# Feed-forward layers of a hybrid encoder block: where the row sums' pieces, the first down product and one weight part stand in the queues

## The chip, the cores and the metric

The kernel runs on one core of one Trainium2 chip. The metric is device time in microseconds (us) of one execution; the kernel before was run three times.

## The reference, cut to what matters

The whole block is a macaron: half a feed-forward layer, a mixer (convolution and gated linear attention), half a second feed-forward layer, and a gated per-layer input. The change touches the two feed-forward layers. In them, for 512 tokens, 1024 channels and an inner width of 2816:

```python
def _swiglu(x, w_in, w_out):
    gate, up = jnp.split(x @ w_in, 2, axis=-1)
    return (jax.nn.silu(gate) * up) @ w_out
h = h + 0.5 * _swiglu(_rmsnorm(h, ffn1_norm[i]), ffn1_w_in[i], ffn1_w_out[i])
...
h = h + 0.5 * _swiglu(_rmsnorm(h, ffn2_norm[i]), ffn2_w_in[i], ffn2_w_out[i])
```

## The kernel before, in words

Every float32 product is done as three matmuls of split operands: with a high part H and a low part L of each side, the kernel adds wH·xH, wH·xL and wL·xH. So every weight tile of 128x1024 values is fetched by SyncE (SP) into a raw tile `wr` (six buffers), cast by ScalarE (ACT) to `wh`, and its rest `wl` = `wr` − `wh` is made in one of two ways. `low` (line 193) makes it with one subtraction on VectorE (DVE). `added` (line 198) makes it without DVE: ACT writes −`wr`, rounded as `wh` is, into `wl` (a second ACT pass) and GpSimd (POOL) issues a DMA that adds `wr` to it in place.

The inner width is worked in pairs of 256 columns (11 pairs of 128-row blocks). Two kinds of pairs exist:

- A plain pair has eight units h0 to h7 on TensorE (PE), each of 12 matmuls of 512 columns. In the first layer pair 1 is plain. Its weight parts a11, a12 (gate) and a21, a22 (up) serve h0 to h3 and h4 to h7; h5 is the first user of a22.
- The others use a scheme with seven products instead of eight: units m1 (a11), m2 (a12), m6 (s2), m7 (s3), m5 (s1), m4 (a22), m3 (s4), each of 24 matmuls of 256 columns. s1 to s4 are sums of the weight parts (`sm` tiles, or written over `wr`), made by DVE. The other side needs sums over the tokens, too: t1 to t4.

Class `Right` (line 325 on) makes the token sums. `steps()` hands out five steps: pieces of `h` times a norm vector on ACT (`xg` tiles, four 128x256 activations a step) and differences of those on DVE. `split` turns the results into `t2H`, `t2L` and so on. Step 0 and 1 run ahead of the layer; steps 2 to 4 and the splits are hung on units as hooks, which run behind the unit's matmuls in program order.

`second(cut)` (line 749) makes the down products for a range of the inner width: four pieces, each of 2 x 12 matmuls of 512 columns with the activations `actH`, `actL` (made by `act_parts`, line 654, of `m`, the gated product of pair 0 and of pair 1) and a part of `w_out`.

The order on PE is the list `units`; `drive` (line 584) walks it. A unit's weight parts are fetched 7 to 9 units ahead and split 4 units ahead (`AHEAD`), or 6 units ahead where the unit stands in `adds`, which also sends its part through `added`. Each engine runs its instructions in the order in which the program issues them, so where a split stands in this walk is where it stands in the queue of ACT or DVE. Behind the plain pair the units before are: m1(2), m2(2), the first down piece, m1(3), m6(2), m7(2), m5(2), m2(3), m4(2), m3(2), the second down piece, m6(3) and so on; the number is that of the pair. All of these matmuls, splits and sums are recorded under line 46, that of a helper.

The second layer has no such list for its opening: lines 1436 to 1457 write it by hand. `plain_block` runs pair 0 as four blocks (g0, u0, g1_, u1_) between which the token sums and the first parts of pair 1 (`w1`) and pair 2 (`w2`) are made:

```python
    xb.split("t2", "t3")
    w1.part("s2")
    w1.add_part("a22")
    w2.add_part("a11")
    w1.s3_()
    u1_ = plain_block(w0, 1, 1)
```

Behind it come m1(1), m2(1), m1(2) and m6(1) on PE; m1(2) is the user of `w2`'s a11.

Of the kernel before, what the change touches and what calls it, by code (L numbers as in the profile page):

```python
# [62 lines left out]
def block_kernel(ctx: ExitStack, tc: tile.TileContext, a: dict, out: bass.AP):  # L63
# [195 lines left out]
    def spread(col, copy=True):  # L259

        ps = aux()
        for j in range(TB):
            pe.transpose(ps[:, j * P:(j + 1) * P], col[:, j:j + 1].to_broadcast([P, P]), ident)
        if not copy:
            return ps
        bc = tmp("bc", bufs=1)
        act.copy(bc, ps)
        return bc
# [245 lines left out]
    w1 = Left(ffn1_in, 2)  # L514
# [35 lines left out]
    xb = Right(hg, "ffn1_norm")  # L550
    steps = xb.steps()
# [4 lines left out]
    def constants():  # L556
        _, cwrow, gwurow = made
        gwu = cp.tile([P, 2 * P], F32, name="gwu")
        act.copy(gwu, gwurow)
        cw = cp.tile([P, 4 * WIDTH], F32, name="cw")  # L560
        ps = aux()
        for c in range(4):
            pe.transpose(ps[:, c * WIDTH:(c + 1) * WIDTH], cwrow[:, c * P:(c + 1) * P], ident[:WIDTH, :WIDTH])
        dve.tensor_copy(cw, ps[:, 0:4 * WIDTH])
        mean = cp.tile([P, P], F32, name="mean")
        pool.memset(mean, 1.0 / D_CONV)
        m1, m2 = (bt(s="m1")[:, 0:4 * CH].rearrange("p (c t) -> p c t", t=CH) for _ in range(2))
        mask = cp.tile([P, 4, CH], I32, name="mask")
        pool.memset(m1, 1.0)
        pool.memset(m2, 1.0)  # L570
        pool.affine_select(out=m1, in_=m1, compare_op=ALU.is_gt, fill=0.0, base=0,
                           pattern=[[0, 4], [-1, CH]], channel_multiplier=1)
        pool.affine_select(out=m2, in_=m2, compare_op=ALU.is_gt, fill=0.0, base=-CH,
                           pattern=[[0, 4], [-1, CH]], channel_multiplier=1)
        pool.tensor_copy(mask[0:CH], m1[0:CH])
        pool.tensor_copy(mask[CH:P], m2[CH:P])
        nbias = cp.tile([P, 2], F32, name="nbias")
        for j in range(2):
            dve.tensor_scalar(nbias[:, j:j + 1], vec("gate_b", j), -1.0, None, ALU.mult)
        made[:] = cw, gwu, mean, mask, nbias  # L580
# [23 lines left out]
    def ffn(w_in, w_out, x, gname, given, first, rsb, hooks, plain, adds=()):  # L604
# [6 lines left out]
        start = 1 + len(plain)  # L611
# [197 lines left out]
        units, had = [], set()  # L809

        def add(kind, i):
            if 0 <= i < npair and (kind, i) not in had:
                had.add((kind, i))
                units.append(unit(kind, i))

        cut_of = {f1 // 2 - 1: (f0, f1) for f0, f1 in CUTS}
        due = []
        for i in plain:
            for j in range(8):
                add(f"h{j}", i)  # L820
                if j in (2, 3, 5, 7):
                    units += due[:1]
                    due = due[1:]
# [1 line left out]
                due += second(cut_of[i])  # L825
        add("m1", start)
        add("m2", start)
        sooner, due = due[:1], due[1:]
        units += sooner
        add("m1", start + 1)  # L830
        for i in range(start, npair):
            add("m6", i)
            add("m7", i)
            add("m5", i)
            if i == end:
                half, rest = second(cut_of[i])
                units.append(half[0])
            else:
                add("m1", i + 1)
            add("m2", i + 1)  # L840
            if not (i == start and sooner):
                units += due[:1]
                due = due[1:]
            add("m4", i)
            add("m3", i)
            units += due[:1]
            due = due[1:]
            if i in cut_of and i < end:
                due += second(cut_of[i])
# [22 lines left out]
    def sums_hooks(x, names, at):  # L872

        h = {}
        for name, key in zip(names, at):
            h[key] = lambda *_, name=name: x.split(name)
        return h

    hooks = sums_hooks(xb, ("t2", "t3", "t1", "t4"), (("h4", 1), ("h5", 1), ("h6", 1), ("m1", 2)))
    hooks.update({("h%d" % (i + 1), 1): f for i, f in enumerate(steps[2:])})  # L880
    hooks.update({("m5", 3): lambda *_: made[0](), ("m5", 4): lambda *_: constants(),
                  ("m4", 10): lambda *_: w_ahead.append(ahead(w_in, D_CONV, 2 * P)),
                  ("last", 4): lambda *_: w_ahead.append(ahead(w_in, 0, 2 * P))})
    hg, norm = ffn(ffn1_in, a["ffn1_w_out"][0], xb, "mix_norm", {0: Left(ffn1_in, 0), 1: w1},
                   (ps0[:2], ps0[2:]), lambda: spread(mid[0]), hooks, (1,),
                   {("h4", 1), ("m1", 2), ("m4", 2)})
    pool.on = False
    cw, gwu, mean, mask, nbias = made

# [89 lines left out]
    for k0 in range(0, DC, 4):  # L979
        for i in range(2):  # L980
            for j in range(4):
                pe.matmul(ps[2 * RANK * j:2 * RANK * (j + 1)], gw[:, k0 + j, :], hg[k0 + j][i].bitcast(F32),
                          start=(k0 == i == 0), stop=(k0 + i == 5), skip_group_check=True)
# [339 lines left out]
    w0, w1 = wf[0], wf[1]  # L1323
# [100 lines left out]
    def plain_block(p, up, i, mid={}):  # L1424
        ps = bank()
        cs = slice(i * P, (i + 1) * P)
        for k in range(DC):
            if k in mid:
                mid[k]()
            wh, wl = p.part(f"a{1 + up}{1 + k // 4}")  # L1430
            mm3(ps, wh[:, k % 4, cs], wl[:, k % 4, cs], *hg[k], k == 0, k == DC - 1)
        return ps

    mid = []
    xb = Right(hg, "ffn2_norm")
    steps = xb.steps()
    steps[0]()
    w1.fetch("a21", "a22")
    w2 = wf[2]
# [8 lines left out]
    w1.s12()  # L1448
    g1_ = plain_block(w0, 0, 1, {1: lambda: mid.append(spread(mid[0]))})
    xb.split("t2", "t3")  # L1450
    w1.part("s2")
    w1.add_part("a22")
    w2.add_part("a11")
    w1.s3_()
    u1_ = plain_block(w0, 1, 1)
    xb.split("t1")
# [1 line left out]
    hooks = sums_hooks(xb, ("t4",), (("m2", 1),))  # L1458
# [3 lines left out]
    q11, q21, q12, q22, b11, b21, t2, wproj = ([] for _ in range(8))  # L1462
# [59 lines left out]
    def todo(*fs):  # L1522
# [6 lines left out]
                  ("rest", 4): todo((q_high, b21, q21, 1), (first_sum, 1), (third_sum, 1)),  # L1529
                  ("rest", 6): todo((final_in,), (row_sums, 0))})  # L1530
    hg, norm = ffn(ffn2_in, a["ffn2_w_out"][0], xb, "ple_norm", wf, ((g0, u0), (g1_, u1_)), mid[1], hooks, ())

    def of_rows(k, h):

        return [tuple(t[:, HS[h]] for t in hg[4 * k + c]) for c in range(4)]

    a11, a12, a21, a22 = of_rows(0, 0), of_rows(1, 0), of_rows(0, 1), of_rows(1, 1)
# [138 lines left out]
    def kept(ps, name, **kw):  # L1678
        o = tmp(name, **kw)
        act.copy(o, ps)  # L1680
        return o
# [20 lines left out]
    t1, t3 = q11, q12  # L1702
    n2_ = [x for jp in range(2) for x in split_rows(n2, jp)]
    project(0)
    m1 = [kept(p_, "sq", bufs=3) for p_ in x_]
# [98 lines left out]
```

## Time and profile before

| | us |
|---|---|
| median of 3 runs (lowest, highest) | 956.53 (956.1, 957.69) |
| the profiled execution's own time | 956.29 |
| its span in the profile | 954.6 |
| PE busy | 935.3 (98%) |
| DVE busy | 763.4 (80%) |
| ACT busy | 483.6 (51%) |

The span runs from the first to the last instruction; 1.69 us of the execution's own time lie around it. Starts are counted from the start of the span. A row of the timeline gives start, duration, engine, line, operation, tiles (numbers left out), shape, count, and in brackets how long the engine sat idle before it and what ended that. A matmul's duration overlaps the next one's, so the distance of starts is what it costs PE.

### The profile page before, as it was taken

To read this page: it belongs to the slowest core of one execution; us is meant where nothing else is said; L and a number is where in the kernel's file an instruction comes from. 1 tells how busy PE (TensorE), PEld (TensorE's weight loads), DVE (VectorE), ACT (ScalarE), POOL (GpSimd) and SP (SyncE) were. 2 spreads that over 40 slices of the span, in tenths; PEclk is the share of its full clock that TensorE was granted. 3 is DMA by queue.
4 is the path that set the end of the run, shared out by engine and by line. 5 is a ranking of instruction groups with operands and counts; after the bars stand their busy time and mean duration, and the time that the engine had idled before them with its cause. 6 is when DMAs were issued, how large, how long until landed. Compare 5 with 4: busy or idle time off the path is not lost.

```text
span 954.6 us, 14724 instructions
## 1 busy us (share of the span) xinstructions
PE 935.3 (98%) x5914; PEld 834.3 (87%) x5914; DVE 763.4 (80%) x1038; ACT 483.6 (51%) x728; POOL 56.9 (6%) x74
## 2 busy tenths in 40 slices
PE   9969999999999999999999999999999999999996
PEld 7859999999999988788877889999999999998885
DVE  6797778877878666999987689887888787865896
ACT  5863443344434473374564775444334443445882
POOL 0100010000000020101020010000000000000131
PEclk9989999999999999999999999999999999999998
DMA  7725232422243395338453554323243224347463
GB/s 227 207 61 154 74 101 92 133 89 90 89 133 94 108 245 131 89 67 200 99 121 112 135 114 128 111 91 104 94 133 102 77 89 133 95 139 225 94 111 110
DMA packets 108120, 114.48 MB, mean 120 GB/s; under 512 B 5187, under 2 KB 96501, under 8 KB 108052
## 3 DMA queue, kind: packets, MB, share of 16 engines
q1 hardware_dynamic: 101732, 94.67, 32.1%
q0 software_dynamic: 6304, 18.88, 11.0%
q8 instruction: 46, 0.75, 0.3%
q14 instruction: 22, 0.18, 0.1%
q10 hardware_dynamic: 16, 0.00, 0.0%
HBM read 93.61 MB, written 2.10 MB: 100 GB/s over the span
## 4 chain that ended last, share of the span: by engine, by line
PE 89%; DVE 4%; DMA 3%; ACT 2%; issue 2%; SPq 1%; POOL 0%; POOLq 0%; DVEq 0%; ACTq 0%
PE ps L46 88%; PE ax L46 1%; DMA wl<-wr 1%; DMA wr<-in_ffn_w_in 1%; DVE xg L46 1%; DVE wl L46 1%; DMA x<-in_x 1%; DVE sqacc L46 1%; ACT xg L46 1%; ACT wh L46 0%; DMA gwurow<-in_gate_w_up 0%; SPq L481 0%; ACT s L46 0%; DVE g L46 0%; SPq L446 0%
## 5 line engine op out<-in xcount | busy, mean ns | idle before, releaser
L46 PE MATMUL ps<-hgH,wl 128*128 128x256 f32 (+1 forms) x768 | 230.6, 305 | 1.4 <-DMA wl<-wr 1.4
L46 PE MATMUL ps<-hgH,wh 128*128 128x256 f32 (+1 forms) x768 | 231.5, 307 | 0.2 <-DVE wh L46 0.2
L46 PE MATMUL ps<-hgL,wh 128*128 128x256 f32 (+1 forms) x768 | 230.8, 306 | 0.0
L46 DVE TENSOR_TENSOR wl<-wr,wh 128x1024 fp32r<-128x1024 f32 (+2 forms) x161 | 188.6, 1182 | 46.6 <-ACT wh L46 46.5
L46 ACT CAST wh<-wr 128x1024 fp32r<-128x1024 f32 (+2 forms) x178 | 178.9, 1020 | 21.4 <-PE ps L46 6.9
L46 PEld LDWEIGHTS ps<-hgH,wh 128*128 128x128 f32 x768 | 146.5, 191 | 8.7 <-issue 1.1
L46 PEld LDWEIGHTS ps<-hgH,wl 128*128 128x128 f32 x768 | 146.7, 191 | 7.9 <-DMA wl<-wr 1.6
L46 PEld LDWEIGHTS ps<-hgL,wh 128*128 128x128 f32 x768 | 146.4, 191 | 6.9 <-issue 0.2
L46 PE MATMUL ps<-actL,wh 128*128 128x512 f32 x352 | 138.5, 394 | 6.5 <-DVE actL L46 6.5
L46 PE MATMUL ps<-actH,wh 128*128 128x512 f32 x352 | 138.6, 394 | 0.9 <-ACT actH L46 0.9
L46 PE MATMUL ps<-actH,wl 128*128 128x512 f32 x352 | 137.9, 392 | 0.0
L46 ACT ACTIVATE s<-g 128x512 f32<-128x512 f32 x48 | 30.4, 633 | 193.8 <-DVE g L46 193.8
L46 PEld LDWEIGHTS ps<-actL,wh 128*128 128x128 f32 x352 | 66.9, 190 | 19.4 <-DVE actL L46 6.8
L46 DVE SCALAR_TENSOR_TENSOR cv<-glu,cw,cv 128x502 f32<-128x502 f32 (+24 forms) x120 | 81.0, 731 | 0.6
L46 PEld LDWEIGHTS ps<-actH,wh 128*128 128x128 f32 x352 | 66.8, 190 | 14.3 <-ACT actH L46 1.3
L46 PEld LDWEIGHTS ps<-actH,wl 128*128 128x128 f32 x352 | 66.7, 190 | 14.1
L46 DVE SCALAR_TENSOR_TENSOR h<-ps,h 128x512 f32<-128x512 f32 x80 | 54.1, 686 | 20.2 <-PE ps L46 20.2
L46 ACT COPY sq<-ps 128x512 f32<-128x512 f32 x42 | 24.5, 586 | 79.6 <-PE ps L46 79.4
L46 DVE TENSOR_TENSOR wl<-sm,wh 128x1024 fp32r<-128x1024 f32 x42 | 51.0, 1220 | 1.8 <-ACT wh L46 1.6
L46 ACT CAST wh<-sm 128x1024 fp32r<-128x1024 f32 x42 | 43.7, 1043 | 5.6 <-DVE sm L46 3.4
L46 DVE TENSOR_TENSOR u<-ps,sq 128x512 f32<-128x512 f32 x19 | 13.1, 691 | 39.3 <-ACT sq L46 39.3
L46 ACT CAST actH<-m 128x512 fp32r<-128x512 f32 x44 | 25.3, 618 | 37.9 <-DVE m L46 37.7
(267 smaller groups left out, 1815.2 us busy)
## 6 DMA issues: line engine op xcount, KB each, us to landing
wr<-in_ffn_w_in SPq DMA_DIRECT2D x84, 512.0 KB
wr<-in_ffn_w_out SPq DMA_DIRECT2D x32, 512.0 KB
wr<-in_w_in SPq DMA_DIRECT2D x20, 512.0 KB
wl<-wr POOLq DMA_DIRECT2D x18, 512.0 KB, 5.6
wr<-in_ffn_w_out SPq DMA_DIRECT2D x16, 384.0 KB
wr<-in_w_out SPq DMA_DIRECT2D x8, 512.0 KB
wq<-in_ple_w_gate SPq DMA_DIRECT2D x8, 512.0 KB
wl<-wq POOLq DMA_DIRECT2D x8, 512.0 KB, 4.6
```

The lines of the kernel that those rows point to most:

```text
L46: inst = call(*args, **kwargs)
```

## The change

In the first layer the units lose the early place of the first down piece: it now stands behind m2(3), like those of later pairs. Steps 2 and 3 of the token sums move to the hook of h0 (they were on h1 and h2), step 4 to h1 (it was on h3), and the splits of t2, t3 and t1 to h2, h3 and h4 (they were on h4, h5, h6). The part a12 of pair 2 goes through `added`, 6 units ahead, as its a11 and a22 did already. In the second layer `w2`'s a11 and `w1`'s a22 are made ahead of s2 of `w1`, and a11 first.

```diff
         add("m1", start)
         add("m2", start)
-        sooner, due = due[:1], due[1:]
-        units += sooner
         add("m1", start + 1)
...
             add("m2", i + 1)
-            if not (i == start and sooner):
-                units += due[:1]
-                due = due[1:]
+            units += due[:1]
+            due = due[1:]
             add("m4", i)
...
-    hooks = sums_hooks(xb, ("t2", "t3", "t1", "t4"), (("h4", 1), ("h5", 1), ("h6", 1), ("m1", 2)))
-    hooks.update({("h%d" % (i + 1), 1): f for i, f in enumerate(steps[2:])})
+    hooks = sums_hooks(xb, ("t2", "t3", "t1", "t4"), (("h2", 1), ("h3", 1), ("h4", 1), ("m1", 2)))
+    hooks.update({("h0", 1): lambda *_: [f() for f in steps[2:4]], ("h1", 1): steps[4]})
...
-                   {("h4", 1), ("m1", 2), ("m4", 2)})
+                   {("h4", 1), ("m1", 2), ("m2", 2), ("m4", 2)})
...
+    w2.add_part("a11")
+    w1.add_part("a22")
     w1.part("s2")
-    w1.add_part("a22")
-    w2.add_part("a11")
     w1.s3_()
```

ACT in the first layer, behind the split of the first activations (`actH`), before. `wr_429` is a22 of pair 1 (for h5), `wr_479` a11 of pair 2:

```order
L46 CAST wh_481<-wr_429 128x1024
L46 ACTIVATE xg_497<-h_97,vcol_93 128x256
L46 ACTIVATE xg_497<-h_98,vcol_93 128x256
L46 ACTIVATE xg_500<-h_97,vcol_93 128x256
L46 ACTIVATE xg_500<-h_98,vcol_93 128x256
L46 CAST wh_508<-wr_479 128x1024
L46 ACTIVATE wl_509<-wr_479 128x1024
L46 ACTIVATE s_515<-g_113_513 128x512
L46 ACTIVATE xg_530<-h_101,vcol_93 128x256
```

The same place now; `wr_429` is still a22 of pair 1 and `wr_495` a11 of pair 2:

```order
L46 ACTIVATE xg_479<-h_97,vcol_93 128x256
L46 ACTIVATE xg_479<-h_98,vcol_93 128x256
L46 ACTIVATE xg_482<-h_97,vcol_93 128x256
L46 ACTIVATE xg_482<-h_98,vcol_93 128x256
L46 ACTIVATE xg_488<-h_101,vcol_93 128x256
L46 ACTIVATE xg_488<-h_102,vcol_93 128x256
L46 ACTIVATE xg_491<-h_101,vcol_93 128x256
L46 ACTIVATE xg_491<-h_102,vcol_93 128x256
L46 CAST wh_497<-wr_429 128x1024
L46 CAST wh_522<-wr_495 128x1024
L46 ACTIVATE wl_523<-wr_495 128x1024
```

All eight pieces now stand ahead of the cast that h5 needs; before, none did.

DVE in the first layer from the split of t2 on, before. `wl_586` is a12 of pair 2 (for m2), `wl_614` the part of `w_out`, `m_619` the product of pair 1:

```order
L46 TENSOR_TENSOR t2L_578<-xg_422,t2H_577 128x512
L46 TENSOR_TENSOR t2L_582<-xg_533,t2H_581 128x512
L46 TENSOR_TENSOR wl_586<-wr_506,wh_585 128x1024
L46 TENSOR_TENSOR t3L_602<-xg_416,t3H_601 128x512
L46 TENSOR_TENSOR t3L_606<-xg_500,t3H_605 128x512
L46 TENSOR_TENSOR sm_609<-wr_537,wr_539 128x1024
L46 TENSOR_TENSOR sm_610<-sm_609,wr_479 128x1024
L46 TENSOR_TENSOR wl_614<-wr_541,wh_613 128x1024
L46 TENSOR_TENSOR u_139_617<-ps_564,bc_454 128x512
L46 TENSOR_TENSOR m_619<-u_139_617,s_515 128x512
```

The same place now; `wl_622` is a11 of pair 3 (for m1(3)), `m_627` the product of pair 1:

```order
L46 TENSOR_TENSOR t3L_576<-xg_482,t3H_575 128x512
L46 TENSOR_TENSOR g_131_579<-ps_531,bc_454 128x512
L46 TENSOR_TENSOR t1L_597<-xg_413,t1H_596 128x512
L46 TENSOR_TENSOR t1L_601<-xg_479,t1H_600 128x512
L46 TENSOR_TENSOR sm_604<-wr_516,wr_518 128x1024
L46 TENSOR_TENSOR sm_605<-sm_604,wr_495 128x1024
L46 TENSOR_TENSOR wr_516<-wr_495,wr_516 128x1024
L46 TENSOR_TENSOR wl_622<-wr_552,wh_621 128x1024
L46 TENSOR_TENSOR u_142_625<-ps_583,bc_454 128x512
L46 TENSOR_TENSOR m_627<-u_142_625,s_529 128x512
```

The subtractions for a12 of pair 2 and for `w_out` have left this stretch of DVE; the token splits, all three weight sums and a11 of pair 3 now stand ahead of `m`.

ACT in the opening of the second layer, before. `wr_5370` is a22 of pair 1, `wr_5372` a11 of pair 2, `sm_5478` s2 of pair 1:

```order
L46 CAST t3H_5525<-xg_5411 128x512
L46 CAST wh_5529<-sm_5478 128x1024
L46 CAST wh_5533<-wr_5370 128x1024
L46 ACTIVATE wl_5534<-wr_5370 128x1024
L46 CAST wh_5538<-wr_5372 128x1024
L46 ACTIVATE wl_5539<-wr_5372 128x1024
L46 CAST t1H_5569<-xg_5362 128x512
```

The same place now; `wr_5373` is a11 of pair 2, `wr_5371` a22 of pair 1, `sm_5479` s2:

```order
L46 CAST t3H_5526<-xg_5412 128x512
L46 CAST wh_5530<-wr_5373 128x1024
L46 ACTIVATE wl_5531<-wr_5373 128x1024
L46 CAST wh_5535<-wr_5371 128x1024
L46 ACTIVATE wl_5536<-wr_5371 128x1024
L46 CAST wh_5540<-sm_5479 128x1024
L46 CAST t1H_5570<-xg_5363 128x512
```

a11 of pair 2 has moved from the last of three to the first, and POOL's two adding DMAs follow in the same new order.

## Prediction

> **What bounds the kernel now.** I read the page first: PE is busy for 98% of the span, so what can be won is PE's idle time and its time at a low clock. The list of waits of PE then says who caused it; two entries are of the stretches that the change touches.
>
> ```profile
> PE 935.3 (98%) x5914; PEld 834.3 (87%) x5914; DVE 763.4 (80%) x1038; ACT 483.6 (51%) x728; POOL 56.9 (6%) x74
> PE ps L46 <- DVE actL L46: 6.5, 1, 6.5
> PE ps L46 <- DMA wl<-wr: 1.4, 1, 1.4
> ```
>
> The timeline of PE shows the first place. The rows are: the third product of h5, two products of the plain pair 17 apart, the first and last product of m1(2) and m2(2), the down piece up to its two waits, and the first product back at full pace.
>
> ```profile
> 46.02 0.39 PE L46 MATMUL ps<-hgH,wl 128*128 128x512 f32 x1
> ...
> 49.65 0.39 PE L46 MATMUL ps<-hgH,wh 128*128 128x512 f32 x1
> ...
> 53.50 0.39 PE L46 MATMUL ps<-hgH,wl 128*128 128x512 f32 x1
> 53.73 0.28 PE L46 MATMUL ps<-hgH,wh 128*128 128x256 f32 x1
> ...
> 59.36 0.28 PE L46 MATMUL ps<-hgH,wl 128*128 128x256 f32 x1
> ...
> 60.64 0.39 PE L46 MATMUL ps<-actH,wl 128*128 128x512 f32 x1
> 61.91 0.50 PE L46 MATMUL ps<-actH,wh 128*128 128x512 f32 x1 [0.88 <-ACT actH L46]
> 68.88 0.80 PE L46 MATMUL ps<-actL,wh 128*128 128x512 f32 x1 [6.47 <-DVE actL L46]
> ...
> 74.45 0.40 PE L46 MATMUL ps<-actH,wl 128*128 128x512 f32 x1
> ```
>
> A product of 512 columns costs (53.50 − 49.65) / 17 = 0.227 us, one of 256 costs (59.36 − 53.73) / 47 = 0.12, so a unit of 24 costs 2.88. At that pace the product of 61.91 was due at 60.87 (1.04 late), the one of 68.88 at 62.14 (6.74 late), and the 13 steps from there to 74.45 took 5.57 instead of 2.95 (2.62 late). The first place costs **10.40**.
>
> The 2.62 are clock: the windows by stretch show it at 0.67 on average while PE waits. With full clock up to some moment and half clock behind it that moment is 64.0.
>
> ```profile
> 50.00:55.00 5.00, 5.00 (x29) 4.34 (x28) 3.55 (x6) 3.98 (x7) 0.00 (x0) 1.00 0.00 1
> 55.00:60.00 5.00, 5.00 (x42) 4.91 (x41) 4.97 (x6) 4.04 (x6) 0.00 (x0) 1.00 0.00 0
> 62.00:68.00 6.00, 0.41 (x1) 0.09 (x1) 5.97 (x10) 1.08 (x2) 0.00 (x0) 0.67 0.38 122
> 574.00:575.00 1.00, 0.06 (x1) 0.00 (x0) 0.76 (x2) 1.00 (x2) 0.00 (x0) 1.00 0.97 224
> ```
>
> Why the activations are late is in DVE's timeline: none of these rows has idle time before it, and `actL` of pair 1 stands behind splits and sums that only later units need.
>
> ```profile
> 58.41 1.22 DVE L46 TENSOR_TENSOR wl<-wr,wh 128x1024 fp32r<-128x1024 f32 x1
> 59.54 0.68 DVE L46 TENSOR_TENSOR u<-ps,bc 128x512 f32<-128x512 f32 x1
> 60.26 0.69 DVE L46 TENSOR_TENSOR m<-u,s 128x512 f32<-128x512 f32 x1
> 60.87 1.28 DVE L46 TENSOR_TENSOR t1L<-xg,t1H 128x512 fp32r<-128x512 f32 x2
> ...
> 63.21 1.22 DVE L46 TENSOR_TENSOR wl<-wr,wh 128x1024 fp32r<-128x1024 f32 x1
> 64.34 1.22 DVE L46 TENSOR_TENSOR wl<-sm,wh 128x1024 fp32r<-128x1024 f32 x1
> ...
> 66.19 0.69 DVE L46 TENSOR_TENSOR m<-u,s 128x512 f32<-128x512 f32 x1
> 66.80 1.42 DVE L46 TENSOR_TENSOR hgL<-xg,hgH 128x256 fp32r<-128x256 f32 x4
> 68.14 1.28 DVE L46 TENSOR_TENSOR actL<-m,actH 128x512 fp32r<-128x512 f32 x2
> ```
>
> By starts, a long DVE step costs 1.13, a short one 0.60, and 0.12 more where it needs the one before; they are readable 1.22 and 0.69 after their start.
>
> **First layer: what the change removes.** The down piece leaves this place, so both waits for `act` and the slow clock go: 10.40. Behind m2(3), 5 units of 2.88 later, its activations are due near 76 and, by the walk below, ready at 71. The question is what PE waits for instead.
>
> **First layer: the new queue.** ACT's prices are read from these rows, POOL's from the two below:
>
> ```profile
> 40.86 1.05 ACT L46 CAST wh<-wr 128x1024 fp32r<-128x1024 f32 x1
> 41.81 1.70 ACT L46 ACTIVATE xg<-h,vcol 128x256 f32<-128x256 f32 x4
> 43.42 1.04 ACT L46 CAST wh<-wr 128x1024 fp32r<-128x1024 f32 x1
> ...
> 51.02 0.63 ACT L46 ACTIVATE s<-g 128x512 f32<-128x512 f32 x1 [2.87 <-DVE g L46]
> 51.55 1.12 ACT L46 CAST t2H<-xg 128x512 fp32r<-128x512 f32 x2
> 52.58 1.05 ACT L46 CAST wh<-wr 128x1024 fp32r<-128x1024 f32 x1
> ...
> 45.73 0.86 POOL L46 DMA_DIRECT2D wl<-wr  x1 [9.19 <-ACT wl L46]
> DMA to landing us min/median/max: 5.0/5.0/5.0
> ```
>
> So 0.95 a long cast, 0.40 a piece, 0.53 a silu, 0.52 a short cast, and 5.0 from POOL's issue to landing; the pass before it ended at 43.42 + 0.95 + 1.05, so POOL issues 0.3 behind ACT. I walk the new order from 40.86, where before the cast for h5 began; nothing ahead of it has moved.
>
> 1. ACT runs eight pieces (8 x 0.40) to 44.1 and casts a22 until 45.15; DVE's subtraction ends at 46.4. h5's third product was at 46.02: it waits **0.5**. Bounds: none, if pieces run at 0.35, to 0.6.
> 2. ACT makes a11 of pair 2 until 47.0 (its DMA lands at about 52.3, needed at 54.4). DVE does three differences and the gate product (0.60, 0.72, 0.60) until 48.9; ACT follows with silu, t2 (2 x 0.52) and the two passes of a12, which end at 52.5. POOL issues 0.3 later, landing is at 57.8. m2(2)'s third product is due at 53.73 + 0.5 + 2.88 + 0.24 = 57.35: it waits **0.5**. Before, DVE had made this part in time; that is the price of the move to POOL. The other row for such a DMA is 7.85 (the chain, below), from a moment with fetches and another adding DMA in flight. I take 5.0, since both windows from 50 to 60 show the DMA idle, and the one fetch that moves ahead (a12 of pair 3, behind DVE's subtraction) starts at 46.4. With 7.85 the wait would be 3.4.
> 3. ACT: t3 until 53.6, silu at 55.0 behind DVE's gate product, t1 until 56.7, cast of a11 of pair 3 until 57.6. DVE: t1 at 56.2 and 56.8, the three sums at 57.4, 58.6, 59.8, then `wl` of a11 at 60.9, ready at 62.1. m1(3)'s third product is due at 57.9 + 2.64 + 0.24 = 60.8: it waits **1.4**. This and the wait before share their cover: a later landing lengthens one and shortens the other, to 3.4 together at the most and 1.9 at the least.
> 4. DVE goes on with u, m, and the splits of s2, s1, s3 at 63.35, 64.5, 65.6. m6(2) needs s2 at 65.1 and has it at 64.6: **0**, with 0.5 of cover; m7(2) and m5(2) have over 1 us. The second `m` ends at 68.2; ACT then casts `actH`, the two passes of a22 and a12 of pair 3 until 71.7, DVE has its rest at 72.9, needed at 73.7: **0**.
> 5. Two dependent gate steps on DVE end at 74.2, ACT's silu and copy at 75.3, the cast of the `w_out` part at 76.3, its rest at 77.6. The down piece's third product is due at 62.2 + 2.64 + 4 x 2.88 + 0.45 = 76.8: it waits **0.8** (none, if step 3 is 0.8 later).
>
> New waits: 0.5 + 0.5 + 1.4 + 0.8 = 3.2, between 2.4 and 4.3. Walked the same way, the old order gives 68.5 for the product of 68.88. From m4(2) on both orders are the same on PE, and no wait of that kind stands in PE's list between there and the second layer, so the time kept stays kept.
>
> **Second layer.** ACT's row of s2 and of the last pass, the chain's piece for the DMA, and PE:
>
> ```profile
> 562.40 1.05 ACT L46 CAST wh<-sm 128x1024 fp32r<-128x1024 f32 x1 [1.46 <-DVE sm L46]
> ...
> 566.20 1.06 ACT L46 ACTIVATE wl<-wr 128x1024 fp32r<-128x1024 f32 x1
> 567.56 7.85 DMA wl<-wr
> 573.78 0.28 PE L46 MATMUL ps<-hgL,wh 128*128 128x256 f32 x1
> 575.45 0.39 PE L46 MATMUL ps<-hgH,wl 128*128 128x256 f32 x1 [1.39 <-DMA wl<-wr]
> 575.67 0.28 PE L46 MATMUL ps<-hgH,wh 128*128 128x256 f32 x1
> ```
>
> m1(2) waits from 573.90 to 575.45, and the next step takes 0.22 instead of 0.12: 1.65. Now a11's two passes take the place in which ACT sat idle for 1.46 (from 560.9) and end at 562.9; POOL issues at about 563.4, and landing is at 568.4 to 571.3 by 5.0 and 7.85: the wait goes, with 2.6 us to spare. What is queued behind: s2's cast. It must wait for a `wh` buffer that u1_ reads until the middle of its 24 products, near 573.66 − 2 x 2.88 − 12 x 0.227 = 565.2, so DVE's subtraction for s2 is done at about 567.5; m6(1) needs it near 576.8, after 9 us of other products. The next sums slip by half a microsecond on DVE and are needed later still. Gain **1.65**, none of it at the least.
>
> **The sum.** Four restarts at 0.1, by the same two rows, add 0.4 to the new waits: 3.6. So 956.29 (the profiled execution's own time) − 10.40 + 3.6 − 1.65 = 947.84, say **947.8**. The median of the runs is 0.24 above that execution; the difference goes into the range. About 0.2% (1.9 us) is what a measurement of this kernel can tell from no change.
>
> **Rivals.**
>
> - *The clock falls again.* Before, it fell at 64.0, 1.6 us after the last product ended, with only one product in the 3 us before. A wait of 1.55 at 573.9 amid products left it at 1.00. If a new wait near 2 us or over drops it, 13 steps again cost 2.6: 950.4. It decides when the m2(2) and m1(3) waits fall together, by a landing past 7 us. [...] I give 0.12.
> - *DVE is the bound, and the wait only changes its name.* DVE is full for 9 us before `actL`, and the order of its work is all that changes; m6(2) has but 0.5 of cover. If DVE runs 3 us later than walked (a long step at the 1.25 of a dependent one, ACT answers late), s2 is late by 2.5: 950.3. Against it: two long steps (a12 of pair 2, the `w_out` part) have left the stretch. 0.09.
> - *The second layer gains nothing* because s2 or t1 becomes the late one: 947.8 + 1.65 = 949.5. 0.04.
> - *Slower than before.* a22 of pair 2 is added by POOL at 71.0, and only its landing frees the raw buffer into which a22 of pair 3 is fetched. The sum s1 of pair 3 waits for that on DVE, ahead of the split of s4 for m3(2). With a landing of 7 and a fetch of 4 (an estimate: it moves the bytes that take 5.0 there) s4 is ready near 85.6, and m3(2) needs it at 85.8: no cost. Each microsecond beyond is one of PE, and past some 3 the clock falls, too (2.6). It ends slower than before by over 1.9 us from 8 us longer than that on: with 8.4, 947.8 + 8.4 + 2.6 = 958.8. No row shows a landing over 7.85. 0.05.
>
> **How the numbers follow.** The forecast has 0.70, at 947.8, between 945.5 (waits of 2.4, restarts hidden, m1(3) helped by faster steps) and 949. The first four cases are faster, 0.95 together; 0.01 of them I leave for two of their losses at once, which ends within 0.2%. The last case is slower, but for 0.01 of its 0.05 in which its delay stays short of that: faster 0.94, within 0.02, slower 0.04. The range 945.3 to 950.8 holds the forecast, the clock case, the second-layer case and most of the DVE case.
>
> **What would show it.** Right: no idle for `actL` at the down piece, which stands near 76; PE rows with waits of half a microsecond at h5 (DVE `wl`) and m2(2) (DMA `wl`), over 1 us at m1(3) (DVE `wl`), under 1 us at the down piece; clock 1.00 from 50 on; no DMA wait in m1(2) of the second layer. Wrong: a clock row under 1.00 between 55 and 80, waits at m6(2) or m3(2), or PE's wait for the adding DMA of a12 over 2 us.

## The result: a little slower, and where the wait went

The changed kernel takes 958.37 us in the median (957.23 to 960.09, 13 runs) against 956.42 for the kernel before, run beside it; the ratio is 1.0023 [1.0014, 1.0031]. The prediction was 947.8, in a range of 945.3 to 950.8, with 0.94 for faster: wrong in size and sign.

TensorE (PE) of the changed kernel, from the page and from its list of waits (columns of the list: who waits, for whom, us in total, times, longest):

```profile
PE 936.5 (98%) x5914; PEld 835.7 (87%) x5914; DVE 762.8 (80%) x1037; ACT 484.9 (51%) x729; POOL 57.7 (6%) x75
PE ps L46 <- ACT u L46: 8.0, 2, 6.1
PE ps L46 <- DVE wl L46: 1.9, 2, 1.7
```

The entries for DVE `actL`, ACT `actH` and the DMA are gone, as forecast. In their place stands one that the kernel before has not at all: PE waits twice for ScalarE's (ACT's) `u`, 8.0 us together. The timeline of PE shows both, and the two waits for a weight's low part. The row of PEld, PE's weight load, is that of m2(2)'s third product:

```profile
46.55 0.39 PE L46 MATMUL ps<-hgL,wh 128*128 128x512 f32 x1
47.21 0.50 PE L46 MATMUL ps<-hgH,wl 128*128 128x512 f32 x1 [0.27 <-DVE wl L46]
...
58.35 0.19 PEld L46 LDWEIGHTS ps<-hgH,wl 128*128 128x128 f32 x1 [0.24 <-DMA wl<-wr]
...
61.22 0.28 PE L46 MATMUL ps<-hgL,wh 128*128 128x256 f32 x1
63.15 0.38 PE L46 MATMUL ps<-hgH,wl 128*128 128x256 f32 x1 [1.65 <-DVE wl L46]
...
71.52 0.28 PE L46 MATMUL ps<-t3H,wl 128*128 128x256 f32 x1
77.86 0.58 PE L46 MATMUL ps<-t1H,wh 128*128 128x256 f32 x1 [6.06 <-ACT u L46]
...
83.15 0.31 PE L46 MATMUL ps<-hgH,wh 128*128 128x256 f32 x1
...
583.93 0.28 PE L46 MATMUL ps<-t3H,wl 128*128 128x256 f32 x1
586.11 0.38 PE L46 MATMUL ps<-t1H,wh 128*128 128x256 f32 x1 [1.90 <-ACT u L46]
```

By starts, with 0.227 and 0.12 as a step at full pace: h5 loses 47.21 − 46.55 − 0.227 = 0.43, m1(3) 1.93 − 0.12 = 1.81, m5(2) 6.34 − 0.12 = 6.22. The 24 products of m5(2) take 83.15 − 77.86 = 5.29 instead of 2.88, another 2.41. The second layer's m5(1) loses 2.18 − 0.12 = 2.06. m2(2) loses 0.20 for the adding DMA of a12, too little for the list. The restarts at h5, m2(2), m1(3) and m5(1) add 0.1 each: the step behind the wait takes 0.33 instead of 0.227 at h5, and 0.22 or 0.23 instead of 0.12 at the others. Together 13.5 come; 10.40 and 1.65 went. That is 1.5 of the 2.2 us between the two spans. Another 0.8 was there before the first changed instruction (the last section), so the account closes to 0.1.

The products slowed at m5(2) are the clock again. Windows of the changed kernel by stretch; the number behind POOL's is the granted clock:

```profile
75.00:76.00 1.00, 0.00 (x0) 0.00 (x0) 1.00 (x2) 0.73 (x2) 0.00 (x0) 1.00 1.03 197
76.00:77.00 1.00, 0.00 (x0) 0.00 (x0) 0.38 (x1) 1.00 (x2) 0.00 (x0) 0.69 0.02 0
77.00:82.00 5.00, 4.14 (x19) 4.14 (x20) 2.94 (x3) 1.76 (x3) 0.00 (x0) 0.50 0.67 209
82.00:84.00 2.00, 2.00 (x14) 2.00 (x13) 1.87 (x2) 0.62 (x2) 0.00 (x0) 0.70 0.01 2
```

What `u` is, the code says. m6 and m5 work in the same PSUM bank `p.x`, and ACT must copy what stands there after m6 (`u2`) before m5 may add to it:

```python
        def m6(p):
            mul(p.x, p.part("s2"), x.op["t2"], False, False)
            p.u2 = snap(p.x, "u2", bufs=1)
        def m5(p):
            mul(p.x, p.part("s1"), x.op["t1"], False, False)
```

m6(2)'s last product started at 68.64; the copy ran at 77.22. ACT's timeline of the changed kernel shows what stood ahead of it in the queue:

```profile
65.47 0.62 ACT L46 CAST actH<-m 128x512 fp32r<-128x512 f32 x1
69.19 0.62 ACT L46 CAST actH<-m 128x512 fp32r<-128x512 f32 x1 [3.10 <-DVE m L46]
69.72 1.05 ACT L46 CAST wh<-wr 128x1024 fp32r<-128x1024 f32 x1
70.67 1.05 ACT L46 ACTIVATE wl<-wr 128x1024 fp32r<-128x1024 f32 x1
71.63 1.03 ACT L46 CAST wh<-wr 128x1024 fp32r<-128x1024 f32 x1
75.27 0.63 ACT L46 ACTIVATE s<-g 128x512 f32<-128x512 f32 x1 [2.62 <-DVE g L46]
75.81 0.57 ACT L46 COPY sq<-ps 128x512 f32<-128x512 f32 x1
76.28 1.05 ACT L46 CAST wh<-wr 128x1024 fp32r<-128x1024 f32 x1
77.22 0.59 ACT L46 COPY u<-ps 128x512 f32<-128x512 f32 x1
```

ACT isn't busy; it is held, for 3.10 us by VectorE's (DVE's) `m` and for 2.62 by its `g`, and the copy, which needs neither, stands behind both. The late `m` and `g` are the same DVE queue that delayed `actL` before. In the second layer it is the same picture: the copy is the second instruction behind a silu that waited 3.79 us for `g`.

```profile
584.47 0.63 ACT L46 ACTIVATE s<-g 128x512 f32<-128x512 f32 x1 [3.79 <-DVE g L46]
585.01 0.57 ACT L46 COPY sq<-ps 128x512 f32<-128x512 f32 x1
585.47 0.59 ACT L46 COPY u<-ps 128x512 f32<-128x512 f32 x1
```

The kernel before has the same two copies, and no wait for them. Its copies and first products of m5(2) and m5(1):

```profile
81.33 0.59 ACT L46 COPY u<-ps 128x512 f32<-128x512 f32 x1 [2.29 <-PE ps L46]
84.02 0.28 PE L46 MATMUL ps<-t1H,wh 128*128 128x256 f32 x1
...
583.19 0.59 ACT L46 COPY u<-ps 128x512 f32<-128x512 f32 x1
583.95 0.28 PE L46 MATMUL ps<-t1H,wh 128*128 128x256 f32 x1
```

There the copy ended 2.1 us ahead of m5(2), which came some 12 us later than in the new order, but only 0.17 us ahead of m5(1).

**The theory** to test: PE's wait wasn't removed but moved, from the activations at the down piece to the copy of `u2` at m5, because ACT works in order and something that waits for DVE stands ahead of the copy. **Rivals**: VectorE as a whole is the bound, so that the wait returns under any name; or one of the other parts (earlier pieces, one more adding DMA) is the cost.

### The profile page after: what moved, and what is told of

It is laid out like the page before. It is cut to its first block, busy times and chain, and to the rows that moved or that the text cites. A ratio compares the mean times of both kernels' runs of the same rounds, so it can differ in the third digit from the quotient of the medians.

```text
span 956.8 us, 14725 instructions
## 1 busy us (share of the span) xinstructions
PE 936.5 (98%) x5914; PEld 835.7 (87%) x5914; DVE 762.8 (80%) x1037; ACT 484.9 (51%) x729; POOL 57.7 (6%) x75
## 4 chain that ended last, share of the span: by engine, by line
PE 92%; DVE 4%; ACT 3%; issue 1%; POOLq 0%; POOL 0%; ACTq 0%; DVEq 0%
PE ps L46 90%; PE ax L46 1%; ACT wh L46 1%; DVE wl L46 1%; DVE g L46 1%; ACT xg L46 1%; ACT s L46 0%; ACT wl L46 0%; DVE m L46 0%; ACT sq L46 0%; DVE sm L46 0%; DVE xg L46 0%; DVE t1L L46 0%; DVE u L46 0%; DVE wr L46 0%
## 5 line engine op out<-in xcount | busy, mean ns | idle before, releaser
L46 PE MATMUL ps<-hgH,wl 128*128 128x256 f32 (+1 forms) x768 | 230.9, 306 | 2.0 <-DVE wl L46 1.9
L46 PE MATMUL ps<-hgH,wh 128*128 128x256 f32 (+1 forms) x768 | 232.5, 308 | 0.0
L46 PE MATMUL ps<-hgL,wh 128*128 128x256 f32 (+1 forms) x768 | 230.9, 306 | 0.0
L46 DVE TENSOR_TENSOR wl<-wr,wh 128x1024 fp32r<-128x1024 f32 (+2 forms) x160 | 187.5, 1182 | 47.5 <-ACT wh L46 47.4
L46 ACT CAST wh<-wr 128x1024 fp32r<-128x1024 f32 (+2 forms) x178 | 179.3, 1021 | 18.7 <-issue 6.7
L46 PEld LDWEIGHTS ps<-hgH,wl 128*128 128x128 f32 x768 | 146.8, 191 | 9.2 <-DVE wl L46 2.5
L46 PEld LDWEIGHTS ps<-hgH,wh 128*128 128x128 f32 x768 | 147.1, 192 | 8.6 <-issue 1.1
L46 PEld LDWEIGHTS ps<-hgL,wh 128*128 128x128 f32 x768 | 146.4, 191 | 6.8 <-issue 0.2
L46 PE MATMUL ps<-actH,wh 128*128 128x512 f32 x352 | 137.5, 391 | 0.0
L46 PE MATMUL ps<-actL,wh 128*128 128x512 f32 x352 | 137.4, 390 | 0.0
L46 PE MATMUL ps<-actH,wl 128*128 128x512 f32 x352 | 136.9, 389 | 0.0
L46 ACT ACTIVATE s<-g 128x512 f32<-128x512 f32 x48 | 30.4, 634 | 200.6 <-DVE g L46 200.6
L46 DVE SCALAR_TENSOR_TENSOR cv<-glu,cw,cv 128x502 f32<-128x502 f32 (+24 forms) x120 | 81.1, 733 | 0.6
L46 PEld LDWEIGHTS ps<-actH,wl 128*128 128x128 f32 x352 | 66.1, 188 | 14.0
L46 PEld LDWEIGHTS ps<-actH,wh 128*128 128x128 f32 x352 | 66.2, 188 | 12.8
L46 PEld LDWEIGHTS ps<-actL,wh 128*128 128x128 f32 x352 | 66.2, 188 | 12.4
L46 DVE SCALAR_TENSOR_TENSOR h<-ps,h 128x512 f32<-128x512 f32 x80 | 54.2, 687 | 19.2 <-PE ps L46 19.2
L46 ACT COPY sq<-ps 128x512 f32<-128x512 f32 x42 | 24.5, 585 | 78.7 <-PE ps L46 78.7
L46 DVE TENSOR_TENSOR wl<-sm,wh 128x1024 fp32r<-128x1024 f32 x42 | 51.0, 1222 | 3.3 <-ACT wh L46 3.1
L46 PE MATMUL ps<-t1H,wh 128*128 128x256 f32 x152 | 44.4, 292 | 8.0 <-ACT u L46 8.0
L46 ACT CAST wh<-sm 128x1024 fp32r<-128x1024 f32 x42 | 43.9, 1046 | 6.0 <-DVE sm L46 3.3
L46 PE MATMUL ps<-t1L,wh 128*128 128x256 f32 x152 | 44.1, 290 | 0.0
```

What stands on the lines that cost most here:

```text
L46: inst = call(*args, **kwargs)
```

## The experiments

In all of them the ratio is to the kernel before on the same chip. The changed kernel itself stands at 1.0023.

### Each half alone

The changed kernel with the three lines of the second layer put back:

```diff
-    w2.add_part("a11")
-    w1.add_part("a22")
     w1.part("s2")
+    w1.add_part("a22")
+    w2.add_part("a11")
```

> The changed kernel without the edit of the second layer. Theory (the wait was moved, not removed: TensorE now waits for ScalarE's copy of u2 ahead of m5, in both layers): the second layer's edit is worth about +0.4 us, since m5(1) there waited 1.90 us for the copy where m1(2) had waited 1.65 us for a transfer; so this kernel takes 957.5 to 958.3, with the transfer's wait of about 1.6 us back at m1(2) and no wait for the copy near 586. The prediction's step (the second layer's edit gains 1.65): 960.0.

Measured: 957.1 us, 1.0006 [0.9998, 1.0015], a little under the range. The kernel before with only those lines changed:

> The kernel before with the edit of the second layer alone. Theory: the wait for the transfer at m1(2) goes (1.65 us) and one of about 1.9 us for ScalarE's copy of u2 comes at m5(1): 956.4 to 957.1, that is 0 to +0.7 us. The prediction's step: 954.8, and no wait at m5(1).

Measured: 957.39 us, 1.0014 [1.0005, 1.0023]. The two halves add up (1.0020 against 1.0023). The second layer's edit costs some 1.3 us, where the prediction had a gain of 1.65, and more than the theory's 0.4. The profiles suggest why: in the first kernel the wait for the transfer is back (1.02 us at m1(2)), in the second m5(1) waits 1.89 for `u`, and in this execution the clock falls 1.3 us behind that wait:

```profile
585.00:586.00 1.00, 0.53 (x4) 0.53 (x5) 1.00 (x1) 1.00 (x2) 0.00 (x0) 1.00 0.00 0
586.00:587.00 1.00, 1.00 (x10) 1.00 (x10) 1.00 (x2) 1.00 (x2) 0.00 (x0) 0.90 0.00 0
587.00:588.00 1.00, 1.00 (x6) 1.00 (x6) 1.00 (x2) 0.31 (x1) 0.00 (x0) 0.50 0.00 0
...
589.00:590.00 1.00, 1.00 (x7) 1.00 (x6) 0.53 (x1) 0.04 (x1) 0.00 (x0) 0.50 1.03 354
590.00:591.00 1.00, 1.00 (x9) 1.00 (x9) 0.42 (x1) 1.00 (x2) 0.00 (x0) 0.90 0.96 288
```

Half clock from 586.8 to 590.2, so 3.4 us, at nearly half the pace: about 1.5 us. In the profile of the changed kernel the same wait (1.90) left the clock at 1.00. With m5(1)'s 2.06 and its restart instead of the 1.65 at m1(2), and such a fall in about half the executions (last section), the edit would cost some 1.3 us; that is an estimate.

### The down piece alone

The kernel before, with only the early down piece removed from the units:

> The kernel before with the first down piece set back, and nothing else of the change. Theory: the waits for actH and actL go and the wait of m5(2) for ScalarE's copy of u2 comes, with waits for a weight's low part at m2(2) and m1(3) since VectorE still makes it: 957 to 960. Rival (the prediction's walk: no wait for u2): 949 to 951.

Measured: 957.57 us, 1.0010 [1.0001, 1.0019]. The waits for `actH` and `actL` are gone, and PE's list has `PE ps L46 <- ACT u L46: 6.5, 1, 6.5` instead. So setting the piece back is by itself enough to exchange the one wait for the other; the earlier pieces and the adding DMA aren't needed for it. The converse is the changed kernel with the down piece alone put back to its early place:

> The changed kernel with the first down piece put back to its old place ahead of the second m1 (pieces for the token sums, adding transfer and second layer as changed). Theory (the pieces for the sums are early either way, and what TensorE waits for at the down piece is VectorE's backlog, which is shorter by the one or two weight subtractions that the adding transfer and the new order take from ahead of actL): the down piece waits 5 to 7 us for actL with a lower clock behind it, no wait for u2 in the first layer, 1.9 us for u2 in the second: 955 to 957.3. Rival (setting the down piece back did nothing either way, the earlier pieces for the sums are the cost): as the changed kernel, 958.4.

Measured: 958.08 us, 1.0017 [1.0008, 1.0026], with the wait for `actL` back (5.3 us against 6.5 in the kernel before), none for `u` in the first layer and 1.9 in the second, where the clock fell in this execution too. The median is above the expected 955 to 957.3; the waits are as expected, and the sum had left out a fall of the clock behind the second one.

### What holds the copy in ACT's queue

Two kernels move instructions on ACT past the copy. In the first, the plain pair's `act_parts` (two ACT casts, two DVE subtractions) runs as a hook of m6(2), behind the copy:

```diff
-                        lambda: act_parts(p) if i else None]
+                        lambda: later.append(lambda: act_parts(p)) if i else None]
...
+        if plain:
+            hooks[("m6", start)] = lambda *_: [f() for f in later]
```

> The changed kernel with the splitting of the plain pair's activations (two ScalarE casts actH, two VectorE subtractions actL) issued behind m6(2) instead of behind the last plain unit, so that ScalarE's casts don't stand ahead of the copy of u2 and VectorE's don't stand ahead of the gate. Theory: g is made 1.3 us sooner, its silu starts near 73, the copy ends near 75.5, m5(2) starts 2.3 us sooner than at 77.86, and the lower clock is shorter by up to 2.6 us: 953.5 to 956.1. Rival (VectorE as a whole is the bound and the wait only takes another name further on): 958.4, with a new wait of over 2 us at m2(3) or at the down piece.

Measured: 955.97 us, 0.9992 [0.9983, 1.0000]; PE's wait is 3.79 us instead of 6.06, as the theory asked. The second moves one instruction, the silu of m2(2)'s gate:

```diff
             def gate0():
-                p.s0 = silu(plus(p.y, p.a, 0, "g1"))
+                g = plus(p.y, p.a, 0, "g1")
+                def rest():
+                    p.s0 = silu(g)
+                if plain and p is pairs[start]:
+                    later.append(rest)
+                else:
+                    rest()
```

> The changed kernel with one ScalarE instruction moved: the silu of m2(2)'s gate is issued behind the copy of u2 instead of ahead of the sq copy and the cast of the down weight. Theory: the three that stand behind it no longer wait for VectorE's g (2.62 us idle); the copy ends near 74.8, m5(2) starts about 3.1 us sooner, its wait is 3.0 us instead of 6.06, and the lower clock that came with the long wait (2.6 us lost) mostly goes: 952.7 to 955.3. Rival (the wait comes back under another name at once, since VectorE is the bound): 958.4 with over 2.5 us of new waits at m2(3), the down piece or m4(2).

Measured: 955.04 us, 0.9988 [0.9979, 0.9996]. ACT's timeline of this kernel:

```profile
70.94 1.03 ACT L46 CAST wh<-wr 128x1024 fp32r<-128x1024 f32 x1
71.87 0.58 ACT L46 COPY sq<-ps 128x512 f32<-128x512 f32 x1
72.35 1.04 ACT L46 CAST wh<-wr 128x1024 fp32r<-128x1024 f32 x1
73.30 0.58 ACT L46 COPY u<-ps 128x512 f32<-128x512 f32 x1
74.59 0.63 ACT L46 ACTIVATE s<-g 128x512 f32<-128x512 f32 x1 [0.71 <-DVE g L46]
```

No idle time is left between the cast and the copy, and PE's wait falls by 3.24 us, from 6.06 to 2.82; the median falls by 3.3 against the changed kernel, near the slow end of the theory's range. The part about the clock held only in half: the fall is still there, but lasts 3.4 us (74.2 to 77.7) instead of 6.8. Both deferrals together:

> The changed kernel with both deferrals of the first layer: the plain pair's activations are split behind m6(2), and the silu of m2(2)'s gate is issued behind the copy of u2. Second layer as changed. Theory: nothing ahead of the copy on ScalarE waits for VectorE any more; the copy comes within 1 us of m6(2)'s end, m5(2) doesn't wait, and the 6.06 us and the lower clock behind them go: 949.5 to 952.5. Rival (VectorE is the bound, the wait comes back at m2(3), the down piece or m4(2)): 954 to 957.

Measured: 952.17 us, 0.9958 [0.9946, 0.9971]: 6.2 us below the changed kernel, though only 5 runs. ACT and PE in it:

```profile
67.08 1.04 ACT L46 CAST wh<-wr 128x1024 fp32r<-128x1024 f32 x1
68.02 0.58 ACT L46 COPY sq<-ps 128x512 f32<-128x512 f32 x1
68.50 1.06 ACT L46 CAST wh<-wr 128x1024 fp32r<-128x1024 f32 x1
69.44 0.59 ACT L46 COPY u<-ps 128x512 f32<-128x512 f32 x1
...
71.23 0.28 PE L46 MATMUL ps<-t3H,wl 128*128 128x256 f32 x1
71.36 0.28 PE L46 MATMUL ps<-t1H,wh 128*128 128x256 f32 x1
```

m5(2) follows m7(2) without a gap, and the clock stays at 1.00 in all windows from 60 to 84. The rival that the wait only returns elsewhere got a small part of its due: a wait of 1.0 us for `u` appears in pair 3, at 101. The theory is shown for the first layer.

### The second layer, and the other parts, with the copy out of the way

The silu of the second layer's m2(1) is deferred in the same way (the condition `plain and` dropped):

> As the kernel with both deferrals, and in the second layer too the silu of m2(1)'s gate is issued behind the copy of u2. Theory: the wait of 1.9 us of m5(1) in the second layer goes, and with it the lower clock that follows it in some executions: 1.9 to 3.5 us below the kernel with both deferrals, and the largest differences between executions become smaller. Rival (VectorE's late gate sets the second layer as well, the wait comes back at m4(1)): 0 to 0.5 us below it.

Measured: 949.41 us (949.36 to 950.15), 0.9931 [0.9919, 0.9944], and the scatter is small, as expected. Of PE's waits in it, those for `u`:

```profile
PE ps L46 <- DVE u L46: 1.0, 2, 0.8
PE ps L46 <- ACT u L46: 1.0, 1, 1.0
```

The wait of m5(1) is gone; 0.85 us of it come back two units later, at 583.5 (m4(1)), as a wait for DVE's `u`. To that extent the rival holds in this layer: DVE's queue is late there whoever waits for it. From this kernel on, three single parts of the change were taken back. First the second layer's order:

> The kernel repaired in both layers, without the second layer's edit of the change (the adding transfer of a11 behind that of a22 again, s2 first). Theory (the edit's gain of 1.0 to 1.65 us is real and was eaten by the wait for u2): the wait for the transfer at m1(2) is back with 1.0 to 1.5 us, and this kernel is that much slower than the repaired one. Rival (the edit is worth nothing, m5(1) is bound by VectorE's gate anyway): within 0.4 us of the repaired one.

Measured: 950.08 us, 0.9931 [0.9920, 0.9943], the same ratio. The rival's time was right: m1(2)'s wait for the transfer is back with 0.97 us, but then DVE's `u` isn't waited for. The transfer and DVE's queue hide each other, and asking for the part sooner gains 0.7 us by the medians and nothing by the ratios. Then the low part of a12, made by DVE again:

> The kernel repaired in both layers, with the low part of m2(2)'s weight made by VectorE again instead of by the adding transfer. Theory (VectorE's backlog matters between 57 and 77 us): one subtraction of 1.22 us more stands ahead of VectorE's queue, TensorE's wait at m2(2) or m1(3) grows by 0.5 to 1.2 us: 949.9 to 950.8. Rival (the backlog is hidden now): as the repaired one within 0.4 us.

Measured: 949.23 us, 0.9928 [0.9913, 0.9942], no difference, as the rival had it. PE waits 1.94 us for DVE at m2(2) (and the clock fell behind it in the profiled execution), where it waited 1.65 at m1(3); the 1.0 us at pair 3 are gone in return. Last, the pieces for the token sums at their old hooks:

> The kernel repaired in both layers, with the pieces for the token sums at the places of the kernel before (two units later). Theory (the early pieces weren't what removed the old waits; the down piece's place was): within 1 us of the repaired one on either side, with the wait of 1.65 us at m1(3) shorter, as it was 0.9 us in all with the old places and the down piece set back. Rival (the early pieces free VectorE for the activations): 1.5 to 3 us slower, with a wait at the down piece for actL.

Measured: 947.82 us (946.88 to 947.88, 4 runs), 0.9906 [0.9893, 0.9918]. This is the fastest of all, and its interval lies just below that of the kernel with the early pieces (0.9919 to 0.9944). So the early pieces cost some 2 us (1.6 by the medians, 2.4 by the ratios), more than either expectation allowed for. DVE's timeline in the changed kernel:

```profile
51.08 1.29 DVE L46 TENSOR_TENSOR t2L<-xg,t2H 128x512 fp32r<-128x512 f32 x2 [1.27 <-ACT t2H L46]
54.03 1.30 DVE L46 TENSOR_TENSOR t3L<-xg,t3H 128x512 fp32r<-128x512 f32 x2 [1.65 <-ACT t3H L46]
...
57.13 1.29 DVE L46 TENSOR_TENSOR t1L<-xg,t1H 128x512 fp32r<-128x512 f32 x2 [1.21 <-ACT t1H L46]
58.34 1.22 DVE L46 TENSOR_TENSOR sm<-wr,wr 128x1024 f32<-128x1024 f32 x1
```

and with the old hooks:

```profile
54.19 1.29 DVE L46 TENSOR_TENSOR t2L<-xg,t2H 128x512 fp32r<-128x512 f32 x2 [1.27 <-ACT t2H L46]
55.40 1.22 DVE L46 TENSOR_TENSOR sm<-wr,wr 128x1024 f32<-128x1024 f32 x1
56.66 1.23 DVE L46 TENSOR_TENSOR sm<-sm,wr 128x1024 f32<-128x1024 f32 x1
57.80 1.29 DVE L46 TENSOR_TENSOR t3L<-xg,t3H 128x512 fp32r<-128x512 f32 x2
```

Put early, each split makes DVE wait for ACT's cast right ahead of it (1.27 + 1.65 + 1.21), and the three weight sums, which need nothing from ACT, stand behind. At the old places a sum lies between, and of these three waits only the first is left; one of 1.76 us for the pieces themselves has come ahead of it, at 50.18. From 47 us to t1's split DVE sits idle for ACT 3.0 us instead of 4.1, and t1's split has gone behind `m`. On PE the wait of 1.65 us at m1(3) goes with it, and so do those at h5 and in pair 3: what PE loses from h5 to pair 3 falls from 4.3 us to 0.6. That execution was 1.6 us later at h5 already than the one it is compared with, so its whole time shows less of it.

One attempt to shorten the wait at m1(3) in another way, with the low part of a11 of pair 3 made by the adding DMA, too (`("m1", 3)` added to the set `adds`):

> The kernel repaired in both layers, with the low part of the second m1's weight also made by the adding transfer, so that VectorE's subtraction of 1.22 us goes from between 61.5 and 62.7 us and ScalarE has one pass of 1.05 us more near 56. Theory: the wait of 1.65 us at that m1 goes if the transfer, issued near 58, lands within some 4 us, and is between 0 and 3 us if it takes 5 to 8 as such transfers did elsewhere: 947.8 to 950.8.

Measured: 948.16 us, 0.9920 [0.9907, 0.9933]. The wait at m1(3) is gone from the trace, and 0.6 us for ACT's `sq` have come; the interval overlaps with that of the kernel without it.

## Why the prediction was wrong, point by point

- **What goes (10.40 and 1.65): right.** No wait for `actL` or `actH` is left at the down piece, and none for a11's transfer at m1(2).
- **h5, 0.5; m2(2), 0.5; m1(3), 1.4: right in kind**, with 0.43, 0.20 and 1.81, each with its restart of 0.1. **The down piece, 0.8**: none at 86, where it now stands, and none either with both copies moved, where it comes at 77.
- **"m7(2) and m5(2) have over 1 us" is the step that failed.** It compared only when the weights were ready. m5(2) needs something else as well: the bank, and so the copy of `u2`. It was the walk's rule that was short: it followed what each unit reads, and not who must first have read the place into which it writes. In step 5 the walk even has ACT's silu and copy end at 75.3 and the cast for the down piece at 76.3, ahead of the copy of `u2`, while PE's m5(2) was walked through from 71. The evidence was in the kernel before: the first product of m5(2) needs ACT's copy there, too. Nothing of it stood in the list of waits, because PE itself came 12 us later. Cost: 6.22 + 2.41 = 8.6 us. That the rule tested on the old order gave 68.5 for 68.88 was no proof: the old order had no such wait to miss.
- **"The next sums slip by half a microsecond on DVE and are needed later still": the same error in the second layer.** The slip was as walked: counted from m1(2)'s first product (573.66 before, 575.41 now), the last step of `g` starts 0.54 later (581.40 and 583.69). But what stands behind `g`, the copy, was not needed later still: it had 0.17 us of room, and only because PE had lost 1.65 at m1(2) before. So the 1.65 came back at m5(1) with the slip on top, less the room: 2.02, for the 2.06 measured. With the copies moved in both layers the edit is worth at most 0.7.
- **The rival of a bound DVE whose wait takes another name** was the nearest, but it put the wait at m6(2) with 2.5 us; it came at m5(2), through ACT's queue, with 6. It had 0.09, and even its time was faster. **The rival on the slow side** (the raw buffer of a22) didn't happen: PE has no wait from 83 on in the first layer.
- **The clock.** The prediction let it fall with a wait near 2 us or over. That held: waits of 1.89 to 1.94 us did it in four of seven profiles. What the waits forecast would have done was right, too: 1.65 us at m1(3) kept 1.00. Its own sign of being wrong, a clock under 1.00 between 55 and 80, came true.
- **That 947.8 turns up again with the old hooks is a coincidence**: that kernel isn't the predicted one. The predicted order with both copies moved takes 949.4. In its trace PE loses 4.3 us from h5 to pair 3, where the walk had 3.6, and 1.1 us in the second layer, so that of the 1.65 only 0.5 are gained. The other terms were near, but not all right.

## What to carry to other kernels

For each instruction that a change makes due sooner, list not only its inputs but what must have been read out of its output (a PSUM bank, a buffer): a semaphore that the old trace never shows as a wait may be covered by just the wait that is to go. Here the copy of `u2`, on no list before, cost 6.06 us. An instruction that needs nothing late but stands in its engine's queue behind one that waits is late with it, as the copy at 77.22 was behind the silu that waited 2.62 us; moving that single silu behind the copy gained 3.3 us, moving the pieces and splits of the token sums forward lost some 2. And a step set early so that it can be done early may only make its engine wait there for the other one: DVE sat idle for ACT 4.1 us with the early splits, 3.0 with the old places.

## What the runs showed of the hardware

**A wait of one length did and did not lower the clock.** The stretches in which the granted clock was 0.50 lasted 3.4 us (586.8 to 590.2 above), 6.8 (76.4 to 83.2 in the changed kernel, from the windows 0.69 and 0.70) or 10.3 (64.0 to 74.3 in the kernel before). The same wait of 1.89 to 1.90 us at m5(1) was followed by a fall in three of the six profiles that have it and by none in the other three; waits of 1.64 to 1.66 at m1(3) never were, in seven profiles; one of 1.94 at m2(2) was, and so were those of 2.82 us and over, in six profiles. What decides between a fall and none behind the same 1.89 us is not shown.

**The same order isn't worked off equally fast.** Of the kernels whose order on PE is the same up to m1(3), the one with the silu moved ends its last product before the wait there at 60.82 us, the one with `act_parts` moved at 62.20 (by PE's busy time in the windows from 60 on: 0.82 from 60 to 62; 2.00 and then 0.34, less the 0.14 behind the wait). That is 1.4 us, as much as half of these experiments were after, and the reason why places in two traces were compared by distances, and times by repeated runs.
